# Query and key blocks of an encoder layer: RMS norms through a GpSimd power, read from the PSUM banks, in a written order

## The chip, the cores and the metric

The kernel runs on one core of one Trainium2 chip. The metric is the device time of one execution in microseconds. The five queues of a core are named as in the profile: PE (TensorE, with PEld for its weight loads), DVE (VectorE), ACT (ScalarE), POOL (GpSimd) and SP (SyncE, here a queue of DMA issues). PSUM, where matmul results arrive, is used as eight banks of 128 x 512 float32.

## The reference

One encoder layer over 1024 tokens (a 16 x 64 grid) of width 1024. What matters here is the projection of the queries and keys, their norm by head, and what follows at once:

```python
u = rms_norm(x, norm1_g[l])
proj = u @ w_in[l]
q, k, v, cb, cc, ch, ga, gb = jnp.split(proj, split_pts, axis=-1)
q = rms_norm(q.reshape(B, S, N_HEADS, HEAD_DIM), q_norm_g[l])      # 8 heads x 64
k = rms_norm(k.reshape(B, S, N_HEADS, HEAD_DIM), k_norm_g[l])
y_a = neighbourhood_attention(q, k, v, rpb[l]) @ w_attn_branch[l]
y_b = short_gated_conv(cb, cc, ch, conv_w[l]) @ w_conv_branch[l]
merged = jax.nn.sigmoid(ga) * y_a + jax.nn.sigmoid(gb) * y_b
x = x + merged @ w_o[l]
h = rms_norm(x, norm2_g[l]) @ w_mlp_in[l]
x = x + jnp.square(jax.nn.relu(h)) @ w_mlp_out[l]
```

with `rms_norm(x, g) = x * rsqrt(mean(x * x) + 1e-6) * g`. Inputs and output are float32.

## The kernel before

Every float32 product is made of three float16 products: an operand is scaled by a power of two and split into a high part (ACT writes it) and a low part, the remainder (DVE writes it). High times high, high times low and low times high are added up in one PSUM bank. A **unit** is such a group of 24 matmuls (8 tiles of the inner dimension x 3) with 512 output columns.

Stages, in PE's order: the values V (eight token blocks of 128), Q (eight units, `todo[0:8]`, blocks in the order 2, 6, 3, 7, 4, 5, 0, 1), K (eight units), then two units of the first convolution chunk (lines 794 to 797), then attention over 64 steps with the rest of the convolution between its matmuls (line 1020), then gates and branches, the output projection and the MLP. The MLP and the gates use a Strassen-like scheme with seven products; for the gates, four **forms** of the normalised input are made from `xt` while Q runs (`sform_rows` on ACT, `sform_sums` with four subtractions and additions on POOL, the split on ACT and DVE) and stored to the DRAM tensor `GS` for later.

The program order on each engine is the order in which the Python code emits instructions. `unit` (line 207) emits its matmuls, then the postponed work of the unit before (`settle`), then advances two sorts of generators: `step` the list `fg` (foreground: the norm of the blocks, `qk_vec`, and the forms, `sforms`), `tick` the list `bg` (background: the weight chunks' `prep`). A weight chunk's `prep` (line 255) squares its raw weights on ACT, sums them (L270, L272 on DVE write a column `ones`, a matmul with that column, L201, adds over the partitions, L204 reads the result), derives the power of two (`pow2_half`) and a scale (L279), and then writes the high parts (L306, ACT) and the low parts (L297, DVE). Each low part that is done frees a raw buffer, and the next raw weights are loaded through SP's queue (L234).

For each block of Q or K, `qk_vec` (line 711) does this: ACT copies the bank to `qs` with the weights' inverse scale (L714), squares it (L715); DVE sums by head (L718); `rstd` (line 401) makes the reciprocal root with five small DVE operations and a square root on ACT (L405 to L414); DVE multiplies (L725; for K also by the scale `sgq`, L722, and by the product of both gains, L728); ACT writes the high part (L732), DVE the low part (L734). Then SP issues a transposing DMA (`finish_qk`, L745) into `QD` or `KD`, which use the memory of `xt` and of the split input `u16`. The banks alternate between two tags (`bank("do"[n % 2])`), of three and two banks. The split results have two buffers (tag `q16`).

The norms of the input rows already use a power on POOL: `rpow` (line 417), with one column each (L420 scales and adds epsilon, L421 raises to -0.5).

The mask for attention is made by `bias_make` (L708 on DVE, L709 on POOL) after units 5 and 6 of Q. The two convolution units take two banks of the tag `o`; the attention scores use the tag `s` (three banks, L937), their first operation on DVE is L951, and L825 copies the convolution's first results off the banks.

Of the kernel before, what the change touches and what calls it, by code (L numbers as in the profile page):

```python
# [10 lines left out]
F32 = mybir.dt.float32  # L11
F16 = mybir.dt.float16
# [40 lines left out]
def encoder_block(ctx: ExitStack, tc: tile.TileContext, x, weights, cols, gqk, rel, masks, out):  # L53
# [22 lines left out]
        return bank("dsodsods"[rc[0] % 8])  # L76


    sc = base.tile([128, 516], F32, name="sc")
    sci = sc.bitcast(I32)  # L80
    area = {"keep": [0, 0, 148], "prep": [148, 148, 244], "tmp": [244, 244, 516]}

    def cols_of(kind, n):
        a = area[kind]
# [6 lines left out]
    def keep(n=1):  # L91
        return cols_of("keep", n)

    def tmp(n=1):
        return cols_of("tmp", n)
# [86 lines left out]
    def apart(mark, n=3, of=units):  # L182
        while of[0] < mark + n and not forced[0]:
            yield WAIT
# [60 lines left out]
    class Chunk:  # L245
# [9 lines left out]
        def prep(self):  # L255
# [5 lines left out]
            if self.kind in "QKCG":  # L261
                self.parts = wsp.tile([128, 2, tot], F16, name="w16_ws", tag="ws")
                for p, (k, w) in enumerate(self.widths):
                    while len(self.raw) <= p:
                        yield WAIT
                    A.activation(self.parts[:, 1, :k * w].bitcast(BF16), self.raw[p][:, :k * w], AF.Square,
                                 accum_out=sc[:, at(rm, p)])
                    spend(0, 300 + k * w * 7 // 8)
                    yield
                V.tensor_reduce(sc[:, a], sc[:, at(rm, 0, n)], axis=AX, op=OP.add)  # L270
                c = ones_col()
                V.tensor_tensor(c, sc[:, a], sc[:, gm2], op=OP.mult)  # L272
# [144 lines left out]
    def rpow(ss, n, y, top):  # L417

        v = tmp()
        G.tensor_scalar(sc[:, v], sc[:, ss], 4.0 ** -top / n, 4.0 ** -top * EPS, op0=OP.mult, op1=OP.add)  # L420
        G.tensor_tensor(sc[:, y], sc[:, v], sc[:, minus_half], op=OP.pow)  # L421
        yield

    def pow2_half(ss, top, s, inv, more=0):
# [53 lines left out]
    turned, formed = set(), [0]  # L478
    SFORM = ((9, 0, 0), (9, 2, 1), (10, 1, 0), (10, 3, 1), (11, 0, 1), (12, 1, 1))

    def sform_rows(n):
        assert n in turned and n + 4 in turned
        for b in (n, n + 4):
            A.activation(xt[:, b], xt[:, b], AF.Copy, scale=sc[:, at(ys, b)])

    def sform_sums(n):
        z = [xt[:, b, c:c + 512] for b in (n, n + 4) for c in (0, 512)]
        for o, a, b, op in ((3, 2, 3, OP.subtract), (2, 0, 2, OP.subtract),
                            (0, 3, 0, OP.subtract), (1, 1, 0, OP.add)):
            G.tensor_tensor(z[o], z[a], z[b], op=op)  # L490

    def sforms():

        for mark, n, split in SFORM:
            yield from apart(mark, 0)
            pair = xt[:, n:n + 5:4]
            if not split:
                sform_rows(n)
                sform_sums(n)
                continue  # L500
            v = wqk.tile([128, 4, 2, 512], F16, name="s16", bufs=3)
            v4 = v.rearrange("p (b h) w c -> p b h w c", b=2)
            f = pair.rearrange("p b (h c) -> p b h c", h=2)
            A.activation(v4[:, :, :, 0], f, AF.Copy)
            yield
            V.tensor_tensor(v4[:, :, :, 1], f, v4[:, :, :, 0], op=OP.subtract)
            fg.append(sform_store(n, v))

    def sform_store(n, v):
        yield from apart(units[0], 1)  # L510
        A.dma_start(GS[:, n], v)
        formed[0] += 1

    def ln_step(b, n=1):
        for _ in range(n):
# [2 lines left out]
    def qk_gain():  # L518
        g = gq[:, 0]
        V.tensor_tensor(g, g, gq[:, 1], op=OP.mult)  # L520
        yield
        yield from gain(g, 11, sgq, isgq)

    def turn_row(b):
        ln_turn(u16[:, ORDER.index(b) % 4], b, UT)
# [164 lines left out]
        ln_step(b, 2)  # L690
        turn_row(b)
    fg.append(qk_gain())
    fg.append(sforms())
    for b in 4, 5:
        v_unit(b, 11)
        step(3)
    settle()
    flush()

    def bias_load(p):  # L700
        t = wbias.tile([128, 2, 3, 128], F32, name="bias")
# [6 lines left out]
        V.scalar_tensor_tensor(te, te, sc[:, cinv], mk[:, 0], op0=OP.mult, op1=OP.add)  # L708
        G.tensor_tensor(m[:, e], te, mk[:, 1], op=OP.add)  # L709

    def qk_vec(ps, inv, kind, res):
        qs = wqk.tile([128, 512], F32, name="qs", bufs=3)
        sq = wqk.tile([128, 512], F32, name="sq", bufs=1)
        A.activation(qs, ps, AF.Copy, scale=sc[:, inv])  # L714
        A.activation(sq, qs, AF.Square)  # L715
        yield
        ss, y = tmp(8), tmp(8)
        V.tensor_reduce(sc[:, ss], sq.rearrange("p (h d) -> p h d", h=8), axis=AX, op=OP.add)  # L718
        yield
        yield from rstd(ss, HD, y, 12 if kind == "q" else 0)  # L720
        if kind == "k":
            V.tensor_scalar(sc[:, y], sc[:, y], sc[:, sgq], None, op0=OP.mult)  # L722
            yield
        q3 = qs.rearrange("p (h d) -> p h d", h=8)
        V.tensor_tensor(q3, q3, sc[:, y][:, :, None].to_broadcast([128, 8, HD]), op=OP.mult)  # L725
        yield
        if kind == "k":
            V.tensor_tensor(q3, q3, gq[:, 0][:, None, :].to_broadcast([128, 8, HD]), op=OP.mult)  # L728
        r = 2 if kind == "q" else 1
        t = wqk.tile([128, 8, 2, r, HD], F16, name=kind + "16", tag="q16")  # L730
        q4 = q3[:, :, None, :].to_broadcast([128, 8, r, HD])
        A.activation(t[:, :, 0], q4, AF.Copy)  # L732
        yield
        V.tensor_tensor(t[:, :, 1], q4, t[:, :, 0], op=OP.subtract)  # L734
        res.append(t)

    q16 = {}
    todo = [("q", b) for b in ORDER] + [("k", b) for b in range(8)]

    def finish_qk(n):  # L740
        kind, b = todo[n]
        while not q16[n]:
            step()
        dst = QD.rearrange("p a e w t -> p (a e w) t") if kind == "q" else KD
        SP.dma_start_transpose(dst[:, :, b * 128:(b + 1) * 128], q16.pop(n)[0].rearrange("p h w r d -> p (h w r d)"))  # L745

    for n, (kind, b) in enumerate(todo):
        ch = cQ if kind == "q" else cK
        if n % 8 == 0:
            push(cK if kind == "q" else cConv[0])  # L750
        ps = bank("do"[n % 2])
        q16[n] = []

        def post(ps=ps, kind=kind, n=n, ch=ch):
            fg.append(qk_vec(ps, ch.inv, kind, q16[n]))
        unit(tok_mms(ps, actU, b, ch, 8, 512, 0), post, 4, 6 if 4 < n < 8 else 3)
        if n == 3:
            forced[0] = True
            while formed[0] < 4:
                step()  # L760
            forced[0] = False
# [8 lines left out]
            SP.dma_start(mk, masks)  # L770
            cneg, cinv = keep(), keep()
            V.tensor_scalar(sc[:, cneg], sc[:, isgq], -(2.0 ** -15), None, op0=OP.mult)
            V.tensor_scalar(sc[:, cinv], sc[:, sgq], 2.0 ** 15, None, op0=OP.mult)
            bias = {0: bias_load(0)}
        if n >= 3:
            finish_qk(n - 3)
        if n in (5, 6):
            bias_make(*bias[0], n - 5)
        if n % 8 == 7:
            flush()  # L780

# [16 lines left out]
    while not q16[15]:  # L798
        step()
    settle()  # L800
    finish_qk(15)
    A.activation(sc[:, warm], sc[:, warm], AF.Exp)
    settle()
    drain()
# [1117 lines left out]
```

## Time and profile before

| | us |
|---|---|
| median of 3 runs | 1204.14 (1203.29 to 1204.56) |
| the profiled execution, its own time | 1205.96 |
| its span in the profile | 1204.2 |
| PE busy in the span | 1190.9 |

The span runs from the first to the last recorded instruction; the execution's own time is 1.8 us longer. The granted clock of PE is 1.00 throughout. The profile's matmul ends are modelled, so PE's idle time is best read from the starts of its units.

How the Q/K stage lies in the span, by the starts on PE's timeline:

| stage | from | to | us |
|---|---|---|---|
| Q, eight units | 55.81 | 97.28 | 41.47 |
| K, eight units | 97.28 | 140.77 | 43.49 |
| two convolution units | 140.77 | 153.53 | 12.76 |

In lines of the profile, `out<-in` names the tile written and the tiles read, `x8` counts instructions, and what stands in brackets is the idle time of the engine just before with the engine and line that ended it.

### The profile page before, as it was taken

Reading aid. Unit: us, or ns where it says so; the run is one execution under the profiler, and the core shown is the slowest. Engines: PE = TensorE matmul, PEld = TensorE weight load, DVE = VectorE, ACT = ScalarE, POOL = GpSimd, SP = SyncE. Lnnn points to the kernel's source line nnn. Section 1 sums busy time; section 2 is a strip of 40 time slices with the busy share of each in tenths; the row PEclk is TensorE's granted clock in tenths of the full one; section 3 lists DMA queues with packets and bytes.
Section 4 is the critical chain, followed back from the end, with each engine's and each line's share of the span. In section 5 each row is a group of like instructions: output and inputs, shape, how many; then the busy total and the mean of one; then the engine's idle time right before and its main releaser. Section 6 shows DMA issues by size and latency. Waiting matters only on the chain.

```text
span 1204.2 us, 16886 instructions
## 1 busy us (share of the span) xinstructions
PE 1190.9 (99%) x6206; PEld 574.7 (48%) x6206; DVE 929.0 (77%) x1721; ACT 763.3 (63%) x1185; POOL 435.1 (36%) x292
## 2 busy tenths in 40 slices
PE   8999999999999999999999999999999999999998
PEld 6444445555444444444468444444444444444444
DVE  6767988988368686877878655545549999999997
ACT  7876679867554555337779778678676744746440
POOL 1641011222311112001004465565567471554662
PEclk9999999999999999999999999999999999999999
DMA  9956746676451211224286545445465926345302
GB/s 284 220 181 139 139 119 134 130 146 120 106 121 68 64 60 52 70 92 188 53 159 185 183 156 192 151 138 193 147 247 201 355 94 223 124 139 194 105 35 105
DMA packets 177250, 174.91 MB, mean 145 GB/s; under 512 B 137744, under 2 KB 138256, under 8 KB 173072
## 3 DMA queue, kind: packets, MB, share of 16 engines
q1 hardware_dynamic: 176592, 169.65, 49.0%
q10 hardware_dynamic: 576, 4.19, 0.8%
q8 instruction: 48, 0.79, 0.3%
q14 instruction: 34, 0.28, 0.1%
HBM read 102.51 MB, written 37.75 MB: 116 GB/s over the span
## 4 chain that ended last, share of the span: by engine, by line
PE 78%; DVE 5%; issue 1%; SPq 1%; ACT 1%; DMA 0%; DVEq 0%; ACTq 0%
PE ps_d L210 28%; PE ps_s L210 24%; PE ps_o L210 17%; PE ps_d L1017 6%; PE ps_o L994 1%; PE ps_s L937 1%; SPq L1088 1%; DVE P L977 1%; DVE w_s L1141 1%; DVE sz L951 1%; DVE sg L1257 0%; DVE w_ws L297 0%; ACT w_s L1145 0%; DMA uT<-gs 0%; DVE sc L317 0%
## 5 line engine op out<-in xcount | busy, mean ns | idle before, releaser
L210 PEld LDWEIGHTS <-ops 128*128 128x128 f16 x1356 | 132.5, 98 | 157.3
L210 PEld LDWEIGHTS <-w 128*128 128x128 f16 x1368 | 132.9, 98 | 139.4
L1017 PE MATMUL ps_d<-uT,w_ws 128*128 128x512 f16 x528 | 123.7, 379 | 0.1
L210 PE MATMUL ps_d<-ops 128*128 128x512 f16 (+1 forms) x528 | 118.3, 374 | 0.0
L1743 ACT ACTIVATE ops<-hf,sc 128x2048 f16<-128x2048 f32 x26 | 52.0, 2000 | 98.2 <-PE ps_o L210 35.5
L210 PE MATMUL ps_s<-ops 128*128 128x512 f16 x492 | 112.9, 379 | 0.0
L1130 POOL TENSOR_TENSOR tsum<-raw 128x512 f32<-128x512 f32 x28 | 46.3, 1668 | 148.8 <-ACT raw L1116 148.7
L1323 POOL TENSOR_TENSOR as<-as 128x512 f32<-128x512 f32 x56 | 77.5, 1385 | 38.9 <-ACT as L1603 35.6
L210 PEld LDWEIGHTS <-w_s 128*128 128x128 f16 x588 | 56.7, 98 | 69.6 <-DVE w_s L1141 1.5
L210 PEld LDWEIGHTS <-uT 128*128 128x128 f16 x528 | 51.4, 98 | 64.0 <-issue 2.3
L210 PE MATMUL ps_d<-u2x,w 128*128 128x512 f16 (+1 forms) x360 | 80.0, 372 | 0.0
L1017 PEld LDWEIGHTS <-w_ws 128*128 128x128 f16 x528 | 51.2, 98 | 54.5 <-DVE cv L839 0.4
L210 PE MATMUL ps_o<-ops 128*128 128x512 f16 x336 | 77.1, 379 | 0.0
L1745 DVE SCALAR_TENSOR_TENSOR ops<-hf,sc,ops 128x2048 f16<-128x2048 f32 x26 | 73.4, 2822 | 4.3 <-ACT ops L1743 4.2
L210 PE MATMUL ps_o<-u2T,w 128*128 128x512 f16 (+1 forms) x324 | 71.7, 371 | 0.0
L1116 ACT ACTIVATE raw<-raw,sc 128x256 f32<-128x256 f32 x172 | 71.0, 494 | 0.9 <-DMA raw<-in_weights 0.9
L1130 POOL TENSOR_TENSOR gsum<-raw 128x512 f32<-128x512 f32 x14 | 19.0, 1377 | 132.3 <-issue 71.3
L1145 ACT ACTIVATE w<-raw,sc 128x512 f16<-128x512 f32 (+1 forms) x28 | 24.6, 927 | 54.0 <-DVE sc L432 54.0
L210 PE MATMUL ps_s<-u2T,w 128*128 128x512 f16 (+1 forms) x252 | 52.7, 359 | 0.0
L1636 DVE TENSOR_TENSOR as<-ps_d,as 128x512 f32<-128x512 f32 (+1 forms) x14 | 9.4, 672 | 55.7 <-ACT as L1655 53.4
L960 ACT ACTIVATE sz<-sz,sc 128x384 f32<-128x384 f32 (+1 forms) x64 | 37.2, 582 | 22.4 <-DVE sc L951 15.0
L306 ACT ACTIVATE w_ws<-raw,sc 128x512 f16<-128x512 f32 (+2 forms) x72 | 40.8, 637 | 14.2 <-DVE sc L279 14.2
(360 smaller groups left out, 2633.5 us busy)
## 6 DMA issues: line engine op xcount, KB each, us to landing
raw<-in_weights SPq DMA_DIRECT2D x88, 512.0 KB, 5.3
hs<-as SPq DMA_DIRECT2D x16, 1792.0 KB, 8.8
hf<-hs SPq DMA_DIRECT2D x26, 1024.0 KB, 7.4
w2x<-in_weights SPq DMA_DIRECT2D x16, 512.0 KB, 8.6
raw<-in_weights SPq DMA_DIRECT2D x16, 384.0 KB, 3.4
xt<-in_x SPq DMA_DIRECT2D x8, 512.0 KB, 8.1
gs<-s ACTq DMA_DIRECT2D x4, 1024.0 KB, 3.9
x<-in_x SPq DMA_DIRECT2D x8, 512.0 KB, 10.1
```

What stands on the lines that cost most here:

```text
L210: T.matmul(ps, l, r, start=a, stop=b)
L306: A.activation(self.parts[:, 0, f + o:f + o + m], self.raw[p][:, o:o + m], AF.Copy, scale=sc[:, c:c + 1])
L937: T.matmul(ps[:, :nb * 128], QD[:, p, e, w, i * 128:(i + 1) * 128], KD[:, 2 * p + e, lo * 128:(lo + nb) * 128], start=w == 0, stop=w == 1)
L951: V.tensor_tensor_reduce(z[:, :d["n"]], d["ps"][:, :d["n"]], bm, sc[:, cneg], 3.0e38, OP.add, OP.min, accum_out=sc[:, d["mx"]])
L960: A.activation(z, z, AF.Exp, scale=-1.0, bias=sc[:, d["mx"]], accum_out=sc[:, d["sm"]])
L1017: T.matmul(ps, l, r, start=a, stop=b)
L1116: A.activation(v, v, AF.Copy, scale=sc[:, at(g, 4 * i + k)])
L1130: G.tensor_tensor(t[:, o], a, b, op=OP.add)
L1145: A.activation(o(0), w, AF.Copy, scale=sc[:, s])
L1323: sub.tensor_tensor(z[o], z[a], z[b], op=op)
L1743: A.activation(P[:, 1, 0], hf, AF.Copy, scale=sc[:, Rs])
L1745: V.scalar_tensor_tensor(P[:, 1, 1], hf, sc[:, Rs], P[:, 1, 0], op0=OP.mult, op1=OP.subtract)
```

## The change

Per block of Q and K:

- The bank is no longer copied. ACT squares it from PSUM (`qk_square`), DVE sums by head (`qk_sum`), POOL scales, adds a guard and raises to -0.5, on 128 x 8 (`qk_power`), and DVE multiplies straight out of the bank (`qk_norm`). The weights' scale cancels in the norm; epsilon is scaled instead (`qk_guard`). The factor `sgq` of K is put into the gains once (`qk_gain`). Five small DVE operations and ACT's square root go.
- The order is written out (`qk_chain`): block n's square, block n-1's high part, block n's sum and power, block n-1's low part, block n's multiplication. `qk_chain(n)` is emitted after the matmuls of unit n+1; the turn of block n-2 after unit n.
- All eight banks are used in turn, `"dsodsods"[n % 8]`. The split results of Q and K have five buffers: two of the tag `q16`, three of the tag `s16`, which the forms use before.
- The forms are emitted at fixed places instead of by generators: form 0's rows and sums and form 2's split within V's last units, form 3's split before Q, the rest in Q's first four units. Their stores go from ACT's queue to SP's.
- K's chunk is pushed after the first Q unit, may go on to its sum one unit earlier (`apart` 2 instead of 3), and all background steps are dealt out by a table, `ticks`; the loads of the masks and the first bias move behind the sixth Q unit, `bias_make` to units 9 and 10.
- Of the two convolution units' banks, the second is now one of the tag `s`. The last block's parts and the last two turns stand between these two units.

```diff
-                yield from apart(units[0], 1 if self.kind == "Q" else 3)
+                yield from apart(units[0], {"Q": 1, "K": 2}.get(self.kind, 3))
...
-    minus_half = keep()
+    minus_half = keep(8)
...
+    v_unit(4, 11)
+    step(3)
+    sform_rows(0)
+    sform_sums(0)
+    sform_split(2)
+    v_unit(5, 11)
+    step(3)
     settle()
     flush()
+    sform_split(3)
+    sform_store(2)
+    drain()
...
+    def qk_square(n, ps):
+        kind, b = todo[n]
+        d = blocks[n] = {"ps": ps, "r": 2 if kind == "q" else 1}
+        d["sq"] = wqk.tile([128, 512], F32, name="sq", bufs=2)
+        A.activation(d["sq"], ps, AF.Square)
+
+    def qk_sum(n):
+        d = blocks[n]
+        d["ss"], d["y"] = tmp(8), tmp(8)
+        V.tensor_reduce(sc[:, d["ss"]], d["sq"].rearrange("p (h d) -> p h d", h=8), axis=AX, op=OP.add)
+
+    def qk_power(n):
+        d, kind = blocks[n], todo[n][0]
+        G.tensor_scalar(sc[:, d["ss"]], sc[:, d["ss"]], 4.0 ** -TOP[kind] / HD, sc[:, guard[kind]],
+                        op0=OP.mult, op1=OP.add)
+        G.tensor_tensor(sc[:, d["y"]], sc[:, d["ss"]], sc[:, minus_half], op=OP.pow)
+
+    def qk_norm(n):
+        d = blocks[n]
+        qs = wqk.tile([128, 512], F32, name="qs", bufs=2)
+        q3, p3 = (v.rearrange("p (h d) -> p h d", h=8) for v in (qs, d["ps"]))
+        V.tensor_tensor(q3, p3, sc[:, d["y"]][:, :, None].to_broadcast([128, 8, HD]), op=OP.mult)
+        if todo[n][0] == "k":
+            V.tensor_tensor(q3, q3, gq[:, 0][:, None, :].to_broadcast([128, 8, HD]), op=OP.mult)
+        d["q4"] = q3[:, :, None, :].to_broadcast([128, 8, d["r"], HD])
+
+    def qk_high(n):
+        d = blocks[n]
+        d["t"] = wqk.tile([128, 8, 2, d["r"], HD], F16, name=todo[n][0] + "16",
+                          **({"tag": "q16"} if n % 5 < 2 else {"tag": "s16", "bufs": 3}))
+        A.activation(d["t"][:, :, 0], d["q4"], AF.Copy)
+
+    def qk_low(n):
+        d = blocks[n]
+        V.tensor_tensor(d["t"][:, :, 1], d["q4"], d["t"][:, :, 0], op=OP.subtract)
...
+    def qk_chain(n, ps):
+        qk_square(n, ps)
+        if n:
+            qk_high(n - 1)
+        qk_sum(n)
+        qk_power(n)
+        if n:
+            qk_low(n - 1)
+        qk_norm(n)
+
+    ticks = (0, 2, 4, 0, 4, 8, 6, 6, 2, 2, 3, 4, 4, 5, 5, 5)
...
     for n, (kind, b) in enumerate(todo):
...
+        ps = bank("dsodsods"[n % 8])
+        unit(tok_mms(ps, actU, b, cQ if kind == "q" else cK, 8, 512, 0), lambda n=n, ps=ps: qk_chain(n, ps), 0, 0)
+        if n == 0:
+            sform_rows(1)
+            sform_store(3)
+            sform_split(0)
+            sform_sums(1, (0, 1))
+            push(cK)
+        if n == 1:
+            sform_store(0)
+            sform_sums(1, (2, 3))
         if n == 3:
+            sform_split(1)
+        if n == 4:
+            sform_store(1)
...
+        for m in (0, 1, 2) if n == 4 else (n - 2,) if n > 4 else ():
+            qk_turn(m)
+        tick(ticks[n])
...
-    first = [bank("o"), bank("o")]
+    first = [bank("o"), bank("s")]
     for half in range(2):
         unit(ch_mms(first[half], actU, half, cConv[0], 8, 384, 0), None, 8, 4)
-        finish_qk(13 + half)
...
+        if half == 0:
+            qk_high(15)
+            qk_low(15)
+            qk_turn(14)
+            qk_turn(15)
```

More of the change, by code (lines that the diff above doesn't have):

```diff
@@ L484, in sform_rows, with sform_sums, sform_split, sform_store @@
             A.activation(xt[:, b], xt[:, b], AF.Copy, scale=sc[:, at(ys, b)])
-    def sform_sums(n):
+    def sform_sums(n, part=range(4)):
         z = [xt[:, b, c:c + 512] for b in (n, n + 4) for c in (0, 512)]
-        for o, a, b, op in ((3, 2, 3, OP.subtract), (2, 0, 2, OP.subtract),
-                            (0, 3, 0, OP.subtract), (1, 1, 0, OP.add)):
+        for i in part:
+            o, a, b, op = ((3, 2, 3, OP.subtract), (2, 0, 2, OP.subtract),
+                           (0, 3, 0, OP.subtract), (1, 1, 0, OP.add))[i]
             G.tensor_tensor(z[o], z[a], z[b], op=op)
[L492 to L512, printed above, removed]
+    halves = {}
+    def sform_split(n):
+        v = halves[n] = wqk.tile([128, 4, 2, 512], F16, name="s16", bufs=3)
+        v4 = v.rearrange("p (b h) w c -> p b h w c", b=2)
+        f = xt[:, n:n + 5:4].rearrange("p b (h c) -> p b h c", h=2)
+        A.activation(v4[:, :, :, 0], f, AF.Copy)
+        V.tensor_tensor(v4[:, :, :, 1], f, v4[:, :, :, 0], op=OP.subtract)
+    def sform_store(n):
+        SP.dma_start(GS[:, n], halves.pop(n))
     def ln_step(b, n=1):
@@ L522, in qk_gain @@
         yield from gain(g, 11, sgq, isgq)
+        V.tensor_scalar(g, g, sc[:, sgq], None, op0=OP.mult)
+        yield
     def turn_row(b):
@@ L737, in encoder_block, with qk_guard @@
-    q16 = {}
-    todo = [("q", b) for b in ORDER] + [("k", b) for b in range(8)]
-    def finish_qk(n):
+    blocks, guard = {}, {}
+    todo = [("q", b) for b in ORDER] + [("k", b) for b in range(8)]
+    def qk_guard(kind, inv):
+        e, i = keep(), tmp()
+        V.reciprocal(sc[:, i], sc[:, inv])
+        mul(i, i, i)
+        V.tensor_scalar(sc[:, e], sc[:, i], 4.0 ** -TOP[kind] * EPS, 1e37, op0=OP.mult, op1=OP.min)
+        V.tensor_scalar(sc[:, e], sc[:, e], 1e-36, None, op0=OP.max)
+        guard[kind] = e
@@ L741, in finish_qk, with qk_turn @@
+    def qk_low(n):
+        d = blocks[n]
+        V.tensor_tensor(d["t"][:, :, 1], d["q4"], d["t"][:, :, 0], op=OP.subtract)
+    def qk_turn(n):
         kind, b = todo[n]
[L742 to L743 removed]
         dst = QD.rearrange("p a e w t -> p (a e w) t") if kind == "q" else KD
[L745 to L756 removed]
+        SP.dma_start_transpose(dst[:, :, b * 128:(b + 1) * 128], blocks.pop(n)["t"].rearrange("p h w r d -> p (h w r d)"))
```

59 lines of the change are left out of this document (13 added, 46 removed).

## The prediction

> **What bounds the kernel now.** First the page, then PE's timeline through the Q/K stage and into attention, then the busy times of the stretch behind it.
>
> ```profile
> span 1204.2 us, 16886 instructions
> ## 1 busy us (share of the span) xinstructions
> PE 1190.9 (99%) x6206; PEld 574.7 (48%) x6206; DVE 929.0 (77%) x1721; ACT 763.3 (63%) x1185; POOL 435.1 (36%) x292
> ```
>
> The span is matmuls back to back; only 13.3 us are left in which PE (TensorE) stands. No edit here removes a matmul, so a gain can come only from PE's pauses, and whatever makes PE wait costs its full length. PE's timeline (start, length, what, and in brackets the idle time before it and who ended it):
>
> ```profile
> 97.28 0.38 PE L210 MATMUL ps_d<-w_ws,uT 128*128 128x512 f16 x1
> 98.60 2.94 PE L210 MATMUL ps_d<-w_ws,uT 128*128 128x512 f16 x12 [0.95 <-DVE w_ws L297]
> 102.07 2.58 PE L210 MATMUL ps_d<-w_ws,uT 128*128 128x512 f16 x11 [0.53 <-DVE w_ws L297]
> 104.49 5.34 PE L210 MATMUL ps_o<-w_ws,uT 128*128 128x512 f16 x24
> 109.67 5.34 PE L210 MATMUL ps_d<-w_ws,uT 128*128 128x512 f16 x24
> ...
> 140.77 5.55 PE L210 MATMUL ps_o<-uT,w_ws 128*128 128x512 f16 x24
> 147.65 5.34 PE L210 MATMUL ps_o<-uT,w_ws 128*128 128x512 f16 x24 [1.33 <-ACT qs L714]
> 153.43 0.16 PE L201 MATMUL ps_d<-ones 128*128 128x1 bf16 x1 [0.44 <-DVE ones L272]
> 153.53 0.38 PE L937 MATMUL ps_s<-kD,qD 128*128 128x256 f16 x2
> ...
> 156.99 0.49 PE L937 MATMUL ps_s<-kD,qD 128*128 128x384 f16 x2
> ```
>
> A unit of 24 matmuls takes 109.67 - 104.49 = 5.18 us, 0.216 each. The first K unit (the ninth of the stage, which so began 8 x 5.18 and one column matmul earlier, at 55.8) took 104.49 - 97.28 = 7.21: **2.03** lost, waiting for the low parts of K's weights. The first convolution unit took 147.65 - 140.77 = 6.88: **1.70** lost, mostly the 1.33 until the last K block's copy L714 had read the bank that the next unit takes. The second took 153.43 - 147.65 = 5.78: **0.60** lost, for the column of the next chunk's sum. Together 4.33 us, the most that the rewritten stage can give. Behind it (PE, weight loads, DVE, ACT, POOL busy; clock):
>
> ```profile
> 153.43:200.00 46.57, 46.43 (x286) 23.07 (x286) 40.62 (x130) 38.97 (x93) 7.56 (x13) 1.00 0.57 124
> ```
>
> PE pauses for only 0.14 of those 46.57 us, so time gained before 153 us is kept.
>
> **The change part by part.** Removed per block: the scaled copy off the bank, five small DVE operations, the square root on ACT. Added per block: two POOL (GpSimd) operations on 128x8, scale plus guard and then the power. DVE's queue becomes: sum, low part of the block before, normalise. The last of these waits for POOL in every block, and all that stands behind it on DVE (K's and the convolution's low weight parts) waits too. The nearest POOL rows:
>
> ```profile
> 28.57 0.19 POOL L420 TENSOR_SCALAR sc<-sc 128x1 f32<-128x1 f32 x1
> 28.85 0.55 POOL L421 TENSOR_TENSOR sc<-sc 128x1 f32<-128x1 f32 x1
> ...
> L421 POOL TENSOR_TENSOR sc<-sc 128x1 f32<-128x1 f32 x8 | 4.7, 583 | 0.7
> ...
> 36.59 1.27 POOL L490 TENSOR_TENSOR xt<-xt 128x512 f32<-128x512 f32 x1 [0.95 <-ACT xt L484]
> ...
> 179.39 0.91 POOL L709 TENSOR_TENSOR biasm<-bias,mk 128x384 f32<-128x384 f32 x1 [0.49 <-DVE bias L708]
> ```
>
> A power of one column takes 0.58, the scale before it 0.28 from start to start. The trace has no power of eight columns. If a column costs no more than in the additions, (1.27 - 0.91) / 128 = 2.8 ns, it takes **P** = 0.58 + 7 x 0.0028 = 0.60; if each costs a whole power, 8 x 0.58 = 4.7. I take 0.60, the row that it is nearest to in size and operation, and keep both ends.
>
> **POOL and DVE do not overlap freely**, and this decides the sum:
>
> ```profile
> 95.27 1.23 DVE L734 TENSOR_TENSOR q<-qs,q 128x1024 f16<-128x1024 f32 x1
> 95.34 1.93 POOL L709 TENSOR_TENSOR biasm<-bias,mk 128x384 f32<-128x384 f32 x1 [21.31 <-DVE sc L410]
> ...
> 96.41 0.88 DVE L102 TENSOR_TENSOR sc<-sc 128x8 f32<-128x8 f32 x1
> ```
>
> The mask addition that took 0.91 alone takes 1.93 when begun beside a low part: it stood until the low part was nearly through, and then the tiny product behind the low part stood until POOL was through, to 97.3. So a low part and a power, which the written order puts side by side, run one after the other, whichever begins. [...]
>
> The durations for a walk through the queues (means in ns; two neighbours follow each other some 0.08 closer than the records' lengths):
>
> ```profile
> L506 DVE TENSOR_TENSOR s<-xt,s 128x2048 f16<-128x2048 f32 x4 | 11.4, 2839 | 8.4 <-ACT s L504 8.4
> L734 DVE TENSOR_TENSOR q<-qs,q 128x1024 f16<-128x1024 f32 x4 | 4.9, 1226 | 2.4 <-ACT q L732 2.4
> L297 DVE SCALAR_TENSOR_TENSOR w_ws<-raw,sc,w_ws 128x512 f16<-128x512 f32 x6 | 4.1, 726 | 0.0
> L718 DVE TENSOR_REDUCE sc<-sq 128x8 f32<-128x512 f32 x6 | 4.1, 685 | 0.6 <-ACT sq L715 0.6
> ...
> L504 ACT ACTIVATE s<-xt 128x2048 f16<-128x2048 f32 x4 | 7.6, 1904 | 3.9 <-POOL xt L490 3.9
> L732 ACT ACTIVATE q<-qs 128x1024 f16<-128x1024 f32 x5 | 5.3, 1054 | 1.6 <-DVE qs L725 1.6
> L306 ACT ACTIVATE w_ws<-raw,sc 128x512 f16<-128x512 f32 x8 | 5.1, 705 | 0.0
> ...
> L578 DVE TENSOR_TENSOR vT<-ps_o,sc x1: 692/692/692, 12.6 to 12.6; 128x512 f32<-128x512 f32 x1
> ```
>
> So: sum 0.61, low part 1.14 for Q and half for K, normalise 0.60 (L578 reads a bank too, so reading banks adds nothing), K's weight low 0.67 and high 0.64, a form's high 1.82, its low 2.25 when undisturbed (twice L734; the 2839 holds waits for POOL), a form sum on POOL 1.22.
>
> *K's weights (was 2.03).* A Q block on DVE: sum 0.61 + scale 0.28 + power 0.68 with its gap + low 1.14 + hand-overs 0.14 + normalise 0.60 = 3.45. Four form sums from 57.5 with one form's low between end at 64.6; the lows of forms 3 and 0, each behind a POOL sum, and the guard bring DVE to 70.3. Block 0 ends at 73.2; block 1, behind two more form sums, at 77.7; K's column at 78.0; block 2 at 81.5; form 1's low 83.8; blocks 3 and 4 at 90.7; K's scale 91.9; its first high part 92.7; two lows 94.0; block 5's square stands behind four high parts, to 95.2; block 5 98.7; six lows 102.7. The last low is due 22 matmuls after 97.28, at 102.0. **New loss 0.8**, and 6 us more per us of P.
>
> *The convolution's first unit (was 1.70).* A K block on DVE: 0.61 + 0.57 + 0.28 + 0.68 + 0.1 + 0.60 + 0.60 (the gain) = 3.45 against PE's 5.18, so DVE, some 6 us late at block 8, is level by block 13. Block 14's square starts at 134.6; sum 135.9; low and power 137.5; normalise and gain 138.8; scale 139.0; first high and low 140.35. That low is due at 139.5 + 0.43: **0.4**. The wait for a bank goes, since the second unit's was free since block 9. If P is over 0.65 DVE isn't level in time, and all fifteen powers of blocks 0 to 14 count: 15 us per us of P.
>
> *The next chunk's column (was 0.60)* leaves DVE at 150.0, and PE wants it at 150.3: **0**.
>
> *A new wait.* The second unit now fills one of the three score banks, so attention's third score waits for its copy off the bank (L825, behind the column's scale and a high pair on ACT), 3.9 us behind the column's matmul by the rows of the walk: 154.3. The third score is due 156.99 - 153.53 = 3.46 behind the first, at 153.8: **0.5**.
>
> *At nothing:* the four form stores move from ACT's queue to SP's, ahead of Q's turns; the last waits for form 1's low at 84, and Q's first turn stands behind it, but ACT needs that turn's buffer only five blocks on, at 98. If this cover failed, ACT's high parts would stand and DVE's lows behind them. Masks and bias load later, with 60 us left. ACT loses a copy per block.
>
> **Sum:** -4.33 + 0.8 + 0.4 + 0.5 = -2.6 to -2.7 on the span of 1204.2. The profiled execution took 1205.96, the median of the runs 1204.14; from that, **1201.4**.
>
> **The rivals.** (A) *Slower:* the power costs by the column. Its place is DVE's queue, its price 15 us for each us of P above 0.65, and from P = 0.8 on the change loses (2.0 + 15 x 0.15 = 4.3). At P = 1.2 it loses 5.9: 1210; at 4.7 some 60. For it: a single column already takes 0.55 where the scale takes 0.19, which is arithmetic and could repeat per column. Against: wide POOL rows are cheap by the column. (B) *The seam takes more:* were the third score's copy as late as in the old trace,
>
> ```profile
> 157.51 1.35 ACT L825 ACTIVATE z<-ps_o,sc 128x512 f32<-128x512 f32 x2
> ```
>
> 158.86 - 153.53 = 5.3 behind the first score against 3.46 due, the new wait is 1.9 and the gain 1.3: 1202.8. Against: DVE reached that work late behind K's last block, which now is earlier. (C) *Hidden anyway:* DVE is 87% busy behind the stage (40.62 of 46.57); if it paces, PE's lead is waited off and 1204.1 stays. Against: PE's 46.43.
>
> **How the numbers follow.** Forecast 0.44 (own range P 0.55 to 0.70: 1200.3 to 1202.5), A 0.39, B 0.12, C 0.05. Low end 1200.0: all but the third score gained (-3.9) and a little of that. High end 1212: A up to P = 1.3; about 0.15 lies beyond. 0.2% is 2.4 us, about what a measurement of this kernel can tell from no change. Faster: most of the forecast, 0.40. Same: its rest, B, C and the bottom of A, 0.26. Slower: 0.34.
>
> **What would show it.** The group of powers 128x8 on POOL: near 0.6 or not settles the forecast against A. PE's wait at the first K unit under 1 us; no wait for a bank at the second convolution unit; one of some 0.5 at the third score, ended by ACT's copy; DVE's normalise waiting for POOL in each block, and low parts that never overlap a power. It is wrong altogether if PE waits inside the Q units, or for a turn of Q or K.

## The result, and the profile after

| | before | after |
|---|---|---|
| median of 4 runs, side by side | 1204.35 us (1203.29 to 1205.56) | 1217.62 us (1217.38 to 1218.53) |
| ratio | | 1.0111, 95% interval 1.0094 to 1.0129 |
| the profiled execution, its own time | 1205.96 | 1217.66 |
| its span | 1204.2 | 1215.8 |
| the stage: first Q matmul to first attention score | 97.72 | 110.80 |

The changed kernel is 13.3 us slower; 1201.4 was forecast, and the measured time lies beyond the range as well. The page of the kernel after (busy time, share of the span, instructions):

```profile
span 1215.8 us, 16814 instructions
## 1 busy us (share of the span) xinstructions
PE 1194.1 (98%) x6206; PEld 575.1 (47%) x6206; DVE 925.7 (76%) x1642; ACT 746.8 (61%) x1151; POOL 471.5 (39%) x324
```

DVE and ACT do less than before, POOL does 36 us more, PE has the same 6206 matmuls. PE's timeline of the kernel after, through the end of Q, K, the convolution units and into attention (start, length, what, in brackets the idle time before and who ended it):

```profile
90.73 5.34 PE L210 MATMUL ps_s<-w_ws,uT 128*128 128x512 f16 x24
97.25 0.38 PE L210 MATMUL ps_d<-w_ws,uT 128*128 128x512 f16 x1 [1.18 <-ACT w_ws L306]
98.04 1.47 PE L210 MATMUL ps_d<-w_ws,uT 128*128 128x512 f16 x6 [0.41 <-DVE w_ws L297]
104.65 6.15 PE L210 MATMUL ps_d<-w_ws,uT 128*128 128x512 f16 x17 [5.15 <-DVE w_ws L297]
110.64 5.34 PE L210 MATMUL ps_s<-w_ws,uT 128*128 128x512 f16 x24
...
141.74 5.34 PE L210 MATMUL ps_s<-w_ws,uT 128*128 128x512 f16 x24
152.61 7.59 PE L210 MATMUL ps_o<-uT,w_ws 128*128 128x512 f16 x24 [5.52 <-ACT w_ws L306]
160.03 5.34 PE L210 MATMUL ps_s<-uT,w_ws 128*128 128x512 f16 x24
...
165.24 0.38 PE L970 MATMUL ps_s<-kD,qD 128*128 128x256 f16 x2
...
168.70 0.49 PE L970 MATMUL ps_s<-kD,qD 128*128 128x384 f16 x2
```

The pauses stand at the same two places as before, only longer. The first K unit was due at 90.73 + 5.18 = 95.91 and the next unit began at 110.64: 9.55 us lost, where it had been 2.03. The first convolution unit was due at 146.92 and ended at 160.03: 7.93 lost, where it had been 1.70. The second convolution unit, the column and the third score (3.46 us behind the first) lose nothing. Together 17.48 us. Before, it was 4.40 by the same starts (2.03, 1.70 and 0.67 at the second convolution unit and its column), so PE loses 13.08 more, which is what the stage grew by (110.80 against 97.72) and all but 0.19 of the 13.27 between the medians.

Who made the weights late is seen on POOL and DVE. The group of the new powers in the stage (count, busy time, mean ns of one, idle before):

```profile
L736 POOL TENSOR_TENSOR sc<-sc 128x8 f32<-128x8 f32 x16 | 29.1, 1820 | 1.3
```

L736 is the power of eight columns: 1.82 us in the mean, three times the 0.60 of the forecast. Three of the 16 are lengthened to 2.5 or more by a low part of DVE; the others take 1.64 to 1.66. Two blocks on POOL's timeline of the kernel after:

```profile
87.17 1.17 POOL L734 TENSOR_SCALAR sc<-sc 128x8 f32<-128x8 f32 x1 [3.62 <-DVE sc L730]
88.43 1.64 POOL L736 TENSOR_TENSOR sc<-sc 128x8 f32<-128x8 f32 x1
91.61 0.28 POOL L734 TENSOR_SCALAR sc<-sc 128x8 f32<-128x8 f32 x1 [1.54 <-DVE sc L730]
91.97 2.67 POOL L736 TENSOR_TENSOR sc<-sc 128x8 f32<-128x8 f32 x1
```

The second of them on DVE's timeline, the low part of the block before and the multiplication:

```profile
91.91 1.23 DVE L755 TENSOR_TENSOR q<-qs,q 128x1024 f16<-128x1024 f32 x1 [0.41 <-ACT q L751]
94.67 0.69 DVE L742 TENSOR_TENSOR qs<-ps_s,sc 128x512 f32<-128x512 f32 x1 [1.53 <-POOL sc L736]
```

And DVE's wait for POOL among the waits, with ACT's wait for the weights' scale (us in total, times, longest):

```profile
DVE qs L742 <- POOL sc L736: 27.9, 16, 2.2
...
ACT w_ws L306 <- DVE sc L279: 9.5, 2, 4.9
```

Undisturbed, the power takes 1.64. Begun beside a low part, it is recorded with 2.67 and ends 94.64 - (91.91 + 1.23) = 1.50 behind the low part: the two ran one after the other, which is called the lock below. In the other block it was the scale that stood (1.17 for 0.28). DVE's multiplication waits for it in all 16 blocks, 27.9 us in total, and K's and the convolution's low parts stand behind that on DVE. So does the scale of the weights (L279): ACT waits for it twice, and the 5.52 that PE's timeline puts down to ACT's high part L306 goes back to DVE in this way.

There is a second thing on the page of windows (length, then busy time of PE, weight loads, DVE, ACT, POOL; granted clock of PE, DMA share, GB/s):

```profile
98.00:104.65 6.65, 1.47 (x6) 0.57 (x6) 3.96 (x6) 6.06 (x10) 2.80 (x2) 0.84 1.09 254
104.65:107.00 2.35, 2.35 (x6) 0.84 (x6) 2.35 (x4) 0.87 (x2) 0.00 (x0) 0.50 0.96 186
107.00:110.64 3.64, 3.64 (x13) 1.36 (x11) 2.64 (x4) 0.00 (x0) 1.95 (x2) 0.67 0.89 283
146.92:152.61 5.69, 0.17 (x2) 0.01 (x1) 3.04 (x9) 0.79 (x3) 2.28 (x2) 0.80 0.25 46
152.61:155.00 2.39, 2.39 (x6) 0.84 (x7) 2.39 (x5) 2.39 (x6) 0.00 (x0) 0.50 0.16 19
155.00:157.50 2.50, 2.50 (x8) 0.91 (x7) 2.50 (x6) 2.50 (x6) 0.00 (x0) 0.57 0.82 259
```

During each long wait PE's granted clock falls to 0.50 (1.00 from 101 to 102 us and 0.50 from 103 to 104; 1.00 from 149 to 150 and 0.50 from 151 to 152) and stays there behind it: six matmuls take 2.35 us where they take 1.30 at 1.00. Before, with pauses of at most 1.33 us in the stage, the clock was 1.00 throughout.

### The profile page after: what moved, and what is told of

Same layout as the page of the kernel before. It is cut to its first block, busy times and chain, and to the rows that moved or that the text cites. A ratio compares the mean times of both kernels' runs of the same rounds, so it can differ in the third digit from the quotient of the medians.

```text
span 1215.8 us, 16814 instructions
## 1 busy us (share of the span) xinstructions
PE 1194.1 (98%) x6206; PEld 575.1 (47%) x6206; DVE 925.7 (76%) x1642; ACT 746.8 (61%) x1151; POOL 471.5 (39%) x324
## 4 chain that ended last, share of the span: by engine, by line
PE 81%; DVE 8%; ACT 5%; POOL 4%; issue 2%; DMA 1%; DVEq 0%; ACTq 0%; SPq 0%; POOLq 0%
PE ps_d L210 27%; PE ps_s L210 24%; PE ps_o L210 17%; PE ps_d L1050 9%; POOL sc L736 2%; PE ps_s L970 2%; PE ps_o L1027 1%; DVE w_s L1174 1%; DVE s L498 1%; POOL sc L734 1%; DVE sc L730 1%; ACT w_ws L306 1%; DVE qs L742 1%; ACT sq L439 1%; DVE w_ws L297 0%
## 5 line engine op out<-in xcount | busy, mean ns | idle before, releaser
L306 ACT ACTIVATE w_ws<-raw,sc 128x512 f16<-128x512 f32 (+2 forms) x72 | 40.7, 637 | 27.9 <-DVE sc L279 27.9
```

Of the source, the lines that this page charges most:

```text
L306: A.activation(self.parts[:, 0, f + o:f + o + m], self.raw[p][:, o:o + m], AF.Copy, scale=sc[:, c:c + 1])
```

## The experiments

The theory at this point: the power's price by the column is the whole cause; it makes DVE late, and the two weight waits (and the lower clock) follow. The rival: something else in the change, the written order, the reads of the banks or the hop to POOL as such, makes DVE late. In all runs the stage is compared from the first Q matmul to the first score, which leaves the scatter of the other parts out. Each ratio is to runs of the kernel before made beside that run (medians 1204.35 to 1205.00):

| run | median us | ratio to before (95%) | stage us | PE lost: first K unit, first conv unit, rest |
|---|---|---|---|---|
| before | 1204.35 | | 97.72 | 2.03, 1.70, 0.67 |
| after | 1217.62 | 1.0111 (1.0094 to 1.0129) | 110.80 | 9.55, 7.93, 0 |
| one column | 1200.26 | 0.9965 (0.9952 to 0.9978) | 93.92 | 0.32, 0.28, 0 |
| four columns | 1207.11 | 1.0017 (1.0008 to 1.0026) | 98.94 | 4.46, 1.17, 0 |
| root on ACT and DVE | 1204.98 | 1.0001 (0.9992 to 1.0010) | 96.62 | 2.52, 0.61, 0.17 |
| fillers | 1217.37 | 1.0106 (1.0090 to 1.0123) | 110.34 | |
| longer filler | 1215.53, one run | | 108.71 | |
| late multiplication | 1205.25 | 1.0002 (0.9993 to 1.0012) | 98.10 | 0, 3.40, 1.38 |
| short root | 1200.45 | 0.9960 (0.9945 to 0.9975) | 93.32 | 0, 0, 0 |
| short root, bank undone | 1199.72, one run | | 93.32 | 0, 0, 0 |
| short root, K undone | 1200.80, one run | | 93.96 | 0.64, 0, 0 |
| before with bank and K | 1206.18 | 1.0009 (1.0000 to 1.0018) | 98.39 | 0, 0, 5.07 |
| before with short root | 1202.83 | 0.9982 (0.9972 to 0.9991) | 97.17 | 2.11, 1.57, 0.18 |
| before again | 1204.66 | 0.9998 (0.9988 to 1.0008) | 97.81 | 2.20, 1.63, 0.67 |

93.32 us is 18 units of 5.18 and three columns without a pause; every other stage without fillers is that and what PE lost.

**One column.**

```diff
+        v, y = at(d["ss"], 0, 1), at(d["y"], 0, 1)
...
-        G.tensor_tensor(sc[:, d["y"]], sc[:, d["ss"]], sc[:, minus_half], op=OP.pow)
+        G.tensor_tensor(sc[:, y], sc[:, v], sc[:, at(minus_half, 0, 1)], op=OP.pow)
...
-        V.tensor_tensor(q3, p3, sc[:, d["y"]][:, :, None].to_broadcast([128, 8, HD]), op=OP.mult)
+        V.tensor_tensor(q2, p2, sc[:, at(d["y"], 0, 1)][:, :, None].to_broadcast([128, 1, 512]), op=OP.mult)
```

> One head's power (128x1) serves all eight heads; the norm of the other seven heads is left out, every other instruction stays. Theory (the power's price by the column makes DVE late, and PE's two long waits follow from that): the power falls from 1.64 to about 0.55 us, DVE's multiplication comes about 1.1 us earlier in every block, PE loses 1 to 2 us in the first K unit and the first convolution unit together instead of 17.5, the granted clock stays 1.00: 15 to 16.5 us less than the changed kernel, 2 to 3.5 us less than the kernel before. Rival (something else in the change, such as the written order, the reads of the banks or the hop to POOL, makes DVE late): most of the 13 us stays, over 1212 us.

Measured: 1200.26, 17.4 us less than the changed kernel. POOL's timeline in one block:

```profile
101.24 1.16 POOL L735 TENSOR_SCALAR sc<-sc 128x1 f32<-128x1 f32 x1 [5.39 <-DVE sc L730]
102.48 0.55 POOL L737 TENSOR_TENSOR sc<-sc 128x1 f32<-128x1 f32 x1
```

The first K unit on PE's timeline, and the unit behind it:

```profile
95.52 5.66 PE L210 MATMUL ps_d<-w_ws,uT 128*128 128x512 f16 x24
101.02 5.34 PE L210 MATMUL ps_s<-w_ws,uT 128*128 128x512 f16 x24
```

POOL works on one column instead of eight, and the multiplication reads one factor for all heads. Of these only the power changes in time (0.55 instead of 1.64): an undisturbed scale takes 0.27 and the multiplication 0.69 in both kernels. All but 0.60 of the 17.48 us are gone. The lock between low part and POOL is still there (the scale takes 1.16 beside a low part), and so are the order, the banks and the hop. The rival (over 1212) is out.

**Four columns.** The same edit with four columns, each for two heads.

> Four heads' powers (128x4), each used for two heads; the norm of the other four heads is left out. The theory: the power takes 0.55 + 3 x 0.156 = 1.02 us if each further column costs the 0.156 us that lie between one and eight columns. By the prediction's slope PE loses 1.5 + 15 x (1.02 - 0.65) = 7 us, 2.7 us more than the kernel before; by a line from 1.2 us lost at 0.65 to 12.4 at 1.64 (17.5 less 5 for the lower clock) it loses 5.4 us, 1 us more than before. So 1205 to 1208 us. Rival (a wide power has one price whatever its width): as the changed kernel, 1217 us.

Measured: 1207.11, a stage 1.22 longer than before's (the traced execution, 1205.11, is the shortest of the ten). A power on POOL's timeline:

```profile
105.37 1.01 POOL L737 TENSOR_TENSOR sc<-sc 128x4 f32<-128x4 f32 x1
```

The first K unit on PE's timeline:

```profile
95.70 1.67 PE L210 MATMUL ps_d<-w_ws,uT 128*128 128x512 f16 x7
100.16 5.34 PE L210 MATMUL ps_d<-w_ws,uT 128*128 128x512 f16 x17 [2.79 <-DVE w_ws L297]
```

The price is a line: 0.55, 1.01 and 1.64 us for one, four and eight columns, 0.156 for each further one. Lost are 5.63 us, between the two estimates (7 and 5.4). From one to eight columns the stage grows by 16.88 us for 1.09 us of power: 15.5 us per us in the mean, but 10.9 between one and four columns (5.02 for 0.46) and 18.8 between four and eight (11.86 for 0.63).

**The root without POOL.**

```diff
-        G.tensor_scalar(sc[:, d["ss"]], sc[:, d["ss"]], 4.0 ** -TOP[kind] / HD, sc[:, guard[kind]],
+        V.tensor_scalar(sc[:, d["ss"]], sc[:, d["ss"]], 4.0 ** -TOP[kind] / HD, sc[:, guard[kind]],
                         op0=OP.mult, op1=OP.add)
-        G.tensor_tensor(sc[:, d["y"]], sc[:, d["ss"]], sc[:, minus_half], op=OP.pow)
+        A.activation(sc[:, d["q"]], sc[:, d["ss"]], AF.Sqrt)
...
             qk_low(n - 1)
+        qk_root(n)
         qk_norm(n)
```

`qk_root` is the reciprocal and the three small operations of lines 410 to 414 before, on DVE.

> The changed kernel with the root made as in the kernel before (scale and guard on DVE, square root on ACT behind the high part of the block before, reciprocal and three small DVE operations behind the low part), so POOL has no part in it and DVE gains five small operations of some 0.16 us; written order, eight banks, five buffers and the sooner K weights stay. Theory: the wait for POOL goes and a Q block on DVE takes 0.61 + 0.16 + 0.3 + 1.14 + 0.64 + 0.60 = 3.5 us, as with a power of 0.6 us: PE loses 1 to 2 us, 2 to 3.5 us less than the kernel before. Rival (the written order itself makes DVE late): over 1210 us.

Measured: the time of the kernel before (1.0001), a stage 1.10 shorter. DVE's timeline between a low part and the multiplication of the same block:

```profile
98.43 0.20 DVE L742 RECIPROCAL sc<-sc 128x8 f32<-128x8 f32 x1
98.66 0.17 DVE L743 SCALAR_TENSOR_TENSOR sc<-sc 128x8 f32<-128x8 f32 x1
98.86 0.17 DVE L102 TENSOR_TENSOR sc<-sc 128x8 f32<-128x8 f32 x1
99.06 0.17 DVE L745 SCALAR_TENSOR_TENSOR sc<-sc 128x8 f32<-128x8 f32 x1
99.26 0.69 DVE L751 TENSOR_TENSOR qs<-ps_o,sc 128x512 f32<-128x512 f32 x1
```

No wait for POOL is left, but the four operations take 99.26 - 98.43 = 0.83 us, since each starts 0.2 behind the last, and a fifth stands before the low part. They lie on DVE's queue like the wait that they replace: DVE works 85.37 of the stage's 96.62 us, and PE still loses 2.52 us at the first K unit. PE loses 3.30 in all where 1 to 2 were expected, and the median shows nothing of the 1.10: the gain was overestimated. The rival (over 1210) is refuted.

**The short root.** What DVE does for the root is cut to one operation; the scale and the guard go into ACT's square root, and the correction step is left out.

```diff
+        A.activation(sc[:, d["q"]], sc[:, d["ss"]], AF.Sqrt, bias=sc[:, guard[kind]], scale=4.0 ** -TOP[kind] / HD)
...
+        V.reciprocal(sc[:, d["y"]], sc[:, d["q"]])
```

> The changed kernel with a root that needs neither POOL nor DVE's small operations but one: ACT takes the square root with the scale and the guard inside it, behind the high part of the block before; DVE takes the reciprocal. Left out is the correction step behind the square root (three small DVE operations), so the factor is only as exact as ACT's square root. Theory (time on DVE's queue per block decides): the scale and the correction, 0.23 + 3 x 0.20 = 0.83 us per block less on DVE than in the run with the whole root, 5 us by the time of K's low parts, so that the 2.28 us wait of the first K unit goes: PE loses 0.3 to 1 us in the stage, 3 to 4 us less than the kernel before, like the run with one column. Rival (the order, not DVE's load, keeps the wait): like the run with the whole root, no change from before.

Measured: 1200.45, ratio 0.9960 (0.9945 to 0.9975), faster than both kernels. The whole stage in one window:

```profile
54.04:147.36 93.32, 93.32 (x437) 42.33 (x436) 73.99 (x136) 60.58 (x102) 17.97 (x12) 1.00 0.66 167
```

PE is busy for all of the 93.32 us. DVE does 73.99 us of work, more than the 72.31 of the changed kernel in its 110.80 us: not DVE's work decided there, but its standing. The run before this one shows the other limit, work on DVE's queue (85.37).

**The multiplication one block later**, so that the power has a block's time (edit: `qk_norm(n - 1)` ahead of `qk_sum(n)`, `qk_low(n - 2)` behind `qk_power(n)`, turns of block n-3).

> The changed kernel with its power of eight columns, but DVE multiplies block n-1 when it sums block n, and writes the low part of block n-2 behind it; turns one unit later. Nothing is left out. Theory (what costs is that DVE stands while POOL works): DVE finds the power done, its wait for POOL goes from 28 us to under 3 us; what stays is the lock where K's low weight parts meet a power, up to 1.9 us in a block: PE loses 1 to 3 us in the stage instead of 17.5, 1 to 3 us less than the kernel before. Rival (low parts and powers exclude each other so fully that the order does not matter): the low parts wait as long as the multiplication did, over 1210 us.

Measured: 1205.25, 12.4 us less than the changed kernel but no gain on the kernel before, where 1 to 3 us were expected; the rival (over 1210) is refuted. The first convolution unit on PE's timeline, and the second:

```profile
140.62 5.57 PE L210 MATMUL ps_o<-uT,w_ws 128*128 128x512 f16 x24 [3.01 <-ACT w_ws L306]
146.03 5.34 PE L210 MATMUL ps_s<-uT,w_ws 128*128 128x512 f16 x24
```

DVE's wait for POOL among the waits of the stage:

```profile
DVE qs L742 <- POOL sc L736: 19.0, 12, 2.2
```

The first K unit loses nothing, so the wait as such was the cost there: what DVE waits for POOL up to K's last six low parts fell from 10.6 to 4.3 us. But 19 us of it stay where under 3 were expected: a DVE that is late has nothing to put between block n's sum and its multiplication, and waits for the power after all; in K's blocks it comes round every 4.5 us against PE's 5.18 and is still late at the convolution.

**Fillers**, for the clock: matmuls that nobody reads, 28 ahead of the first K unit and 24 ahead of the first convolution unit.

```diff
+    def filler(ps, m):
+        for i in range(m):
+            T.matmul(ps, actU(0, i % 8)[:, :128], actU(0, i % 8)[:, :512], start=i == 0, stop=i == m - 1)
```

> The changed kernel with matmuls that nobody reads put ahead of the first K unit (28) and of the first convolution unit (24), into the bank that the unit then starts afresh: PE works where it stood for 5 to 6 us. Theory (the granted clock of 0.50 behind the two waits comes from the wait itself): the clock stays 1.00, the K unit's last matmuls are paced by the low parts at 0.67 us each and end near 108.6 us instead of 110.6, the convolution unit near 158 instead of 160: some 4 us less than the changed kernel. Rival (the clock falls for another reason, or the matmuls behind the wait are paced by their weights anyway): no change from the changed kernel, or slower by the filler.

Measured: the unit behind the first K unit began at 108.34 instead of 110.64, with the clock at 1.00, as the theory said, and yet the time stayed (1217.37). PE's timeline at the convolution:

```profile
144.63 5.34 PE L774 MATMUL ps_o<-uT 128*128 128x512 f16 x24
152.47 7.26 PE L210 MATMUL ps_o<-uT,w_ws 128*128 128x512 f16 x24 [2.50 <-ACT w_ws L306]
159.56 5.34 PE L210 MATMUL ps_s<-uT,w_ws 128*128 128x512 f16 x24
```

The windows of the same unit, with the clock behind the POOL column:

```profile
152.47:155.00 2.53, 2.48 (x9) 0.93 (x10) 2.53 (x5) 2.53 (x6) 0.00 (x0) 0.81 0.14 30
155.00:157.50 2.50, 2.50 (x8) 0.89 (x6) 2.50 (x6) 2.50 (x5) 0.04 (x1) 0.51 0.82 277
```

The unit started when its weights were there (152.47, and 152.61 without fillers): what PE won at K it waited off here, because DVE, not PE, set that moment. And a wait of 2.50 us was enough for another low phase, which began some 1.5 us behind it. So the clock went with the wait at both places, and the gain of 4 us did not come (0.25 by the medians).

> The run with fillers again, with 36 instead of 24 ahead of the convolution, 7.8 us from 144.6 to 152.4, as long as the wait for the weights lasts. With 24 PE still stood 2.50 us, the clock fell to 0.51 some 1.5 us behind that wait, and the unit took 7.1 us instead of 5.2. If the fall follows from a pause of 2.5 us or more, the clock now stays 1.00 and the first score comes 1.5 to 2 us sooner than in that run; if the unit is paced by its low parts (0.57 us each, three matmuls are 0.65) or the clock falls for another reason, nothing changes.

With 36 instead of 24 fillers PE no longer stands there, and the clock stays 1.00; its timeline:

```profile
143.80 7.93 PE L774 MATMUL ps_o<-uT 128*128 128x512 f16 x36
151.75 5.58 PE L210 MATMUL ps_o<-uT,w_ws 128*128 128x512 f16 x24
157.16 5.34 PE L210 MATMUL ps_s<-uT,w_ws 128*128 128x512 f16 x24
```

The unit took 157.16 - 151.75 = 5.41, the stage is 1.63 shorter than with 24 and 2.09 shorter than without. By this one run the lower clock cost 2.1 of the 13.1 us; the rest is DVE's lateness.

**The two small lines, undone under the short root.** First the bank (`first = [bank("o"), bank("o")]`), then K's sum (3 units instead of 2).

> The run with the short root, in which PE had no pause left in the stage, with one line undone: both convolution units take banks of the tag o, as in the kernel before. In the changed rotation these two banks were last those of K's blocks 2 and 5 (todo 10 and 13), read some 10 us earlier. Theory: eight banks in turn and the multiplication straight from the bank already took away the wait of 1.33, the line itself is worth nothing: no wait, the stage as long as with the line (93.3 us from the first Q matmul to the first score, within 0.2). Rival (the line carries the 1.33): 94.5 us or more, with a wait for a bank at the second convolution unit.

The stage is 93.32 as with the line, which is thus worth nothing here. Whether the rotation of the banks or the direct reading took the wait away was not separated.

> The run with the short root, K's sum held back to 3 units as in the kernel before. Theory: the column of K's sum goes through PE one unit later (near 85 us instead of 79.9), K's scale leaves DVE near 94.8 instead of 89.6 and the six last low parts start near 101 instead of 95.8, where PE wants the first of them at 97: PE waits 3 to 5 us in the first K unit, some of it with the clock at 0.50 behind, 4 to 6 us longer than the run with the short root, about the time of the kernel before. Rival (the shorter chains alone suffice, as DVE has time to spare): under 1 us longer.

Measured: only 0.64 longer, where 4 to 6 were expected; the rival (under 1) held. K's low parts on DVE's timeline:

```profile
96.19 5.38 DVE L297 SCALAR_TENSOR_TENSOR w_ws<-raw,sc,w_ws 128x512 f16<-128x512 f32 x8
```

The first K unit on PE's timeline, behind its first matmul:

```profile
96.99 5.23 PE L210 MATMUL ps_d<-w_ws,uT 128*128 128x512 f16 x23 [0.38 <-DVE w_ws L297]
```

All eight low parts come in a row, one each 0.67 us, and PE uses one each three matmuls, 0.65 us: a start only just in time is enough. With a DVE that is not late, K's sooner sum is worth 0.64 us.

**The two small lines alone, in the kernel before.**

> The kernel before with two of the change's lines alone: K's chunk may go on to its sum one unit sooner (2 instead of 3), and the second convolution unit's bank is of the score banks' tag. Norms, their order, banks of Q and K and buffers stay as before. If these two lines carry what can be gained, the first K unit loses 0.3 us or less instead of 2.03 and the bank's wait of 1.33 goes: 2 to 3.5 us less than the kernel before. Rival (what is waited for next is just behind): the column of the next chunk's sum, which left DVE at 153.38 in the trace of before, does not come sooner, so that its wait takes up what the bank gave, and the third score waits 1.9 us for its bank: 0 to 1 us less.

Measured: 1206.18, 1.2 us more than the kernel before beside it (1205.00), and a stage 0.67 longer. Neither the 2 to 3.5 us of the theory nor the rival's 0 to 1 us were gained. PE's timeline in the middle of Q:

```profile
78.34 0.16 PE L201 MATMUL ps_s<-ones 128*128 128x1 bf16 x1 [2.95 <-DVE ones L272]
78.36 6.92 PE L210 MATMUL ps_d<-w_ws,uT 128*128 128x512 f16 x24
```

The first K unit and the first convolution unit lose nothing any more, and a new wait takes their place: the column of K's sum now stands in PE's queue sooner than DVE, still busy with a form's low part, can write it. PE waits 2.95 us in the middle of Q, and the next unit runs with the lower clock (85.11 - 78.36 = 6.75). The sooner sum does not pay by itself.

**The short root alone, in the kernel before** (the correction's three operations left out, everything in its place).

> The kernel before with its correction step left out of the norms of Q and K (three small DVE operations per block of 8 columns, some 0.5 us; the places in the order stay). Theory (in the kernel before K's low parts wait for their turn in the order and for K's scale, not for DVE's time): PE's pauses stay near 4.3 us and the time is the same within 1.2 us; the written order is what turns less DVE work into time. Rival (less DVE work alone does it): 3 to 4 us less, as in the run with the short root.

PE's wait for the copy off the bank stays as it was:

```profile
145.62 5.34 PE L210 MATMUL ps_o<-uT,w_ws 128*128 128x512 f16 x24 [1.33 <-ACT qs L717]
```

PE loses 3.86 us and the stage is 0.55 shorter: in the stage, less DVE work alone does not do it. In the run with the short root it came with the rest of the change, of which the written order, the direct reading and the rotation of the banks were not taken apart. The median is lower by 1.83, though, more than the stage shows, more than the theory's 1.2 and less than the rival's 3.

> The kernel before, unchanged, against itself, because the stage from the first Q matmul to the first score accounts for only 0.55 of the 1.83 us by which the run of the kernel before with the short root came out lower. If the rest is scatter of the start and of the later stages, this run gives a ratio within 0.001 of 1, a stage of 97.7 us within 0.1, and a first Q matmul that may lie anywhere from 53.7 to 55.8 us. If instead the start of Q near 55.8 belongs to the kernel before, the short root really made the start sooner, and the ratio is within 0.0005 of 1 with Q starting at 55.5 or later.

The stage lies between 53.93 and 151.74 on PE's timeline. It is 97.81 long (97.72 in the first trace), but Q begins at 53.93 instead of 55.81: the start scatters by some 2 us from execution to execution, the stage by 0.1. The ratio is 0.9998 (0.9988 to 1.0008). Where the other 1.3 us of the run with the short root came from is open.

## Why the prediction was wrong, point by point

- **The step that failed is the price of the power**: "I take 0.60, the row that it is nearest to in size and operation". It takes 1.64, as a further column costs 156 ns, not the 2.8 of an addition. The row for one column was right (0.55); its growth was borrowed from another operation. Rival A named this, with a chance of 0.39, and its own rule gives for 1.64 a loss of 2.0 + 15 x (1.64 - 0.65) = 16.9 against 17.48 measured. The range ended at P = 1.3.
- **The place was right, the slope only in the mean.** DVE's queue, the first K unit and the first convolution unit were named; 15 us per us was forecast, 15.5 measured between one and eight columns. That the 16.9 of rival A's rule comes so near to 17.48 is partly luck: the rule knows no lower clock, and without its 2.1 us PE lost 15.4 and the slope is 13.6.
- **With a price near the assumed one the gain came**: one column (0.55) gave 1200.26 and a stage 3.8 us shorter, somewhat more than the forecast 2.7. The new losses at K and at the convolution were 0.32 and 0.28 where 0.8 and 0.4 were said.
- **The lock was right**: a power beside a low part took 2.67 for 1.64, the scale 1.17 for 0.28, and DVE waited for POOL in each block.
- **The bank's wait went, as said**, but the line that the prediction named has no part in it. **The column** cost 0, as said.
- **The third score's 0.5 was wrong**: it started at its time, 3.46 behind the first, in every run of the changed order (in the kernel before with the bank line, 0.15 late). In the kernel after, the bank that was to hold it up was being copied from 168.31 to 169.04, and the score began at 168.70: it uses another bank.
- **K's sooner sum** is in the prediction's walk (K's column at 78.0) without a price of its own; with the short root it is worth 0.64.
- **The lower clock was not foreseen**: 2.1 us.

## What to carry to other kernels

Price a wide instruction of an unusual function by a row of the same function at another width; one row gives no slope, and a single column that is already dear (0.55 against 0.19 for the scale) is a warning. By the line through 0.55, 1.01 and 1.64, 0.16 of that 0.55 is the column and 0.39 is paid once. An engine that is busy for 72.31 of 110.80 us, like DVE in this stage, can still set the end if it stands in each block: multiply a new wait by the number of blocks before the next deadline. A step made sooner moves its own inputs' deadline too: in the kernel before, K's sooner sum put the wait into PE's queue.

## What was not expected of the hardware

A power on POOL cost 0.156 us for each further column of 128 rows (0.55, 1.01 and 1.64 us for one, four and eight columns), 56 times the 2.8 ns per column by which two additions of the kernel before differ (1.27 us for 512 columns, 0.91 for 384). In these runs it is the function that costs, not the width: the scale on POOL took 0.27 for one column and for eight.

PE's clock fell to 0.50 for spells of 3.4 us or of the double. In the kernel after, in windows of half a us from 97 to 112 and from 146.5 to 160.5 us, the clock is 1.00 or 0.50 but for the windows in which a spell begins or ends (0.56 and 0.62, 0.84 and 0.83). With these two values alone, the mean of a window gives the time at 0.50 as an estimate. In the kernel after, by the windows above: 5.69 x 0.40 + 2.39 + 2.50 x 0.86 = 6.8 us at the convolution and 6.65 x 0.32 + 2.35 + 3.64 x 0.66 = 6.9 at K; in the run with fillers 2.53 x 0.38 + 2.50 x 0.98 = 3.4. Pauses of 2.50 (fillers), 2.79 (four columns, clock 0.50 from 100.16 to 103.16) and 2.95 us (the kernel before with bank and K, 0.50 from 78.34 to 80.00) brought such a spell. One of 2.28 (the root on ACT and DVE) and one of 3.01 (the late multiplication) left the clock at 1.00. With the 2.50 the spell began only 1.5 us after the pause, at 155.00 - 0.96 = 154.04, when PE was back at its matmuls. So the length of a pause alone does not tell; how a pause must lie to bring a spell was not tested.
